# Projecting the first token group from unnormalised x, with the first convolution tap on ScalarE and history copies on GpSimd

## The chip, the cores and the metric

The kernel runs on one core of a Trainium2 chip. The metric is device time in microseconds of one execution. One execution was also recorded by the hardware profiler; its busy times, waits and clocks are what the rows below show. TensorE (PE) multiplies, VectorE (DVE), ScalarE (ACT) and GpSimd (POOL) compute elementwise, SyncE (SP) issues most DMAs, and ScalarE issues the others.

## The reference, cut to what matters

One layer of a hybrid encoder for 2048 prompt tokens and 8 x 16 sample tokens, 17 tiles of 128 tokens in all, width 1024, float32:

```python
h = rmsnorm(x, norm_mix_pre)              # x * rsqrt(mean(x*x)) * gain
P = h @ w_in                              # 3592 columns: q,k,v | z | b,a | B,C,H
qkv = silu(causal_dwconv(P[q,k,v], conv_prev, conv_qkv_w))      # 4 taps
q, k = l2norm(q) * 128**-0.5, l2norm(k)   # per head, 4 heads of 128
beta, g = sigmoid(b), -exp(a_log) * softplus(a + dt_bias)
o, S = gated_delta_rule(q, k, v, g, beta, S0)                   # scan over the tokens
o = rmsnorm(o, gdn_norm_w) * silu(z)
y = B * causal_dwconv(C * H, sc_prev, conv_sc_w)                # 3 taps
x = x + rmsnorm(concat(o, y) @ w_o, norm_mix_post)
x = x + rmsnorm(swiglu(rmsnorm(x, norm_ffn_pre)), norm_ffn_post)
```

The row factor `rsqrt(mean(x*x))` is one number per token, so it can be applied to a token's row of x or to its row of `x*gain @ w_in`. The outputs are the layer's x, the last rows before the convolutions (the history of the next call) and the state S.

## The kernel before, in words

The first stage goes over the tokens in six groups of up to three tiles (`GROUPS`): the first holds prompt tiles 0 and 1 and the sample tile 16. Tokens lie along the free dimension (384 columns), channels along the partitions. Matmuls keep float32 accuracy by a split: x and each weight have a high part, rounded to the fast matmul type, and a low part, the rest; `mm3` (L136) multiplies high by high, low by high and high by low. One projection (`project`) of 128 output channels is 8 x 3 matmuls of 384 columns into one of three PSUM banks (`psd`), and a group has 28 of them: 4 k, 4 v, 4 q, 4 z, and four times C, H, B of the short convolution.

`x_first` (L214 ff.) makes the parts of x for the first group: it loads eight blocks of 128 channels, squares them on ScalarE and VectorE in turn (L227, L229), adds pairs (L232) and sums them over the partitions with one-column matmuls (L234). `rstd` takes the power -0.5 on GpSimd (L130), and `spread` (L171 ff.) turns the row factors into a tile `rb` that has them in all partitions, through a matmul with ones (L178) and a copy (L180). Then each block is multiplied by `rb` (L240), its high part is written by ScalarE with the gain as scale (L243) and its low part by VectorE (L244). Later groups use `x_prep`, which the change leaves as it is.

Weights come through `fetch` and `weights` (L327 ff.). In the first group a raw weight is loaded in two halves (`wr`, three buffers); ScalarE casts each half (L338), GpSimd subtracts for the first half's low part and VectorE for the second's (L340), and the split weight (1 MB, three buffers) is stored to HBM (L343). Later groups load it ready made (L332). Seven of the 28, those with `j % 4 == 3`, are split again in the second group and stored only then; in the last group every second weight is split from raw.

`conv_qkv` (L369 ff.) is the 4-tap convolution: the last three columns of the group before (`hist`) are copied ahead of the projection's columns in a tile R, ScalarE copies the columns out of PSUM, `hist` is renewed from R's end, the tap of weight 3 starts `acc`, and `taps` (L367) adds the other three. The sample tile has its own tile Rs with eight streams of 16 tokens and its own history. A SiLU on ScalarE ends it. `sc_stage` (L448 ff.) does the like with two copies of history and three taps. `gate_prep` (L249 ff.) computes decay and beta for the group, `pair_stage` the k k^T and q k^T blocks and a serial ladder of small products on VectorE, `level_stage`, `chunk_stage` and `sample_stage` the scan.

After the six groups come the output projection and the feed-forward, which the change leaves as they are. The order on each engine's queue is set by a planner: it simulates the program written below in order and places each instruction by the time its inputs are expected, so an instruction can stand well ahead of or behind its place in the text. Each engine takes its own queue strictly in that order.

Of the kernel before, what the change touches and what calls it, by code (L numbers as in the profile page):

```python
# [9 lines left out]
F32 = mybir.dt.float32  # L10
# [15 lines left out]
NS = 8  # L26
# [9 lines left out]
NPD, NPT, NPG = 3, 2, 2  # L36
NR, NKV = 3, 3
# [32 lines left out]
def kernel(  # L70
# [44 lines left out]
    nc.scalar.dma_start(out=cst[:, 0:256], in_=consts[:, 0:256])  # L115
# [25 lines left out]
    with ExitStack() as ph:  # L141
# [30 lines left out]
        def spread(r, n):  # L172
            c = n * P
            rg = small.tile([P, W1], F32, tag="rg", name="rg", bufs=1)
# [4 lines left out]
            rb = small.tile([P, W1], F32, tag="rb", name="rb", bufs=1)  # L179
            A.copy(rb[:, :c], ps[:, :c])  # L180
            return rb
# [33 lines left out]
        def x_first(tiles):  # L215
# [3 lines left out]
            ps = tbank()  # L219
            for k in range(KD):  # L220
                raw = ubuf[k] if k < len(ubuf) else gp.tile([P, H, P], F32, tag="dt", name="dt", bufs=2 * MAXT)
                raw = raw.rearrange("p h c -> p (h c)")[:, :c]
                raws.append(raw)
                (nc.sync if k < 6 else nc.scalar).dma_start(out=raw, in_=xs0[k])
                xk = cp.tile([P, W1], F32, tag="xk", name="xk", bufs=3)
                if k % 2:
                    V.tensor_mul(xk[:, :c], raw, raw)  # L227
                else:
                    A.activation(xk[:, :c], raw, AF.Square)  # L229
                sqs.append(xk)  # L230
                if k % 2:
                    V.tensor_add(xk[:, :c], xk[:, :c], sqs[k - 1][:, :c])  # L232
                    for i in range(n):
                        T.matmul(ps[:, 2 * i:2 * i + 1], xk[:, i * P:(i + 1) * P], ones[:, 0:1], start=(k == 1 and i == 0),  # L234
                                 stop=(k == KD - 1 and i == n - 1), skip_group_check=True)
            r = rstd(small, ps[:, :2 * n].rearrange("p (t c) -> p t c", c=2)[:, :, 0], n, 1.0 / D, EPS, "x")
            rb = spread(r, n)
# [10 lines left out]
            return hi, lo  # L248

        def gate_prep(tiles, hi, lo):  # L250
# [6 lines left out]
            A.activation(bsb[:, :c], ps[:16, :c], AF.Identity, scale=gsct[:, 0:1], bias=gbia[:, 0:1])  # L257
# [111 lines left out]
        def conv_qkv(tiles, ci, ps, dst):  # L369
# [6 lines left out]
            if npr:  # L376
                R = cp.tile([P, 3 + W1], F32, tag="R", name="R", bufs=NR)
                V.tensor_copy(R[:, 0:3], hist[:, ci, :])
                A.copy(R[:, 3:3 + pc], ps[:, :pc])
                V.tensor_copy(hist[:, ci, :], R[:, pc:pc + 3])  # L380
                V.tensor_scalar_mul(acc[:, :pc], R[:, 3:3 + pc], w[:, 3:4])
                taps(acc[:, :pc], lambda d: R[:, d:d + pc], w, 4, pc)
            if npr < n:
                Rs = cp.tile([P, NS, 3 + LS], F32, tag="Rs", name="Rs")
                V.tensor_copy(Rs[:, :, 0:3], cch[:, ci])
                A.copy(Rs[:, :, 3:], ps[:, pc:c].rearrange("p (s l) -> p s l", s=NS))
                V.tensor_copy(cch[:, ci], Rs[:, :, LS:LS + 3])
                V.tensor_scalar_mul(acc[:, pc:c].rearrange("p (s l) -> p s l", s=NS), Rs[:, :, 3:], w[:, 3:4])
# [9 lines left out]
        def qkv_stage(tiles, hi, lo, gt, pool):  # L398
# [6 lines left out]
            for h in range(H):  # L405
                raw = cp.tile([P, W1], F32, tag="kvT", name="kraw", bufs=NKV)
                conv_qkv(tiles, 4 + h, project(h, hi, lo, c), raw)
# [14 lines left out]
            for h in range(H):  # L422
                raw = cp.tile([P, W1], F32, tag="kvT", name="vraw", bufs=NKV)
                conv_qkv(tiles, 8 + h, project(4 + h, hi, lo, c), raw)
# [5 lines left out]
            for h in range(H):  # L430
                o = pool.tile([P, W1], F32, tag="qT", name="qT", bufs=H)
                conv_qkv(tiles, h, project(8 + h, hi, lo, c), o)
# [7 lines left out]
        def z_stage(tiles, hi, lo, gt):  # L440
            c = len(tiles) * P
            sz = gp.tile([P, H, W1], F32, tag="sz", name="sz")
            for h in range(H):
                ps = project(12 + h, hi, lo, c)
                A.activation(sz[:, h, :c], ps[:, :c], AF.Silu)
            gt["sz"] = sz

        def sc_stage(tiles, hi, lo):  # L448
# [4 lines left out]
            for b in range(4):  # L453
# [3 lines left out]
                A.copy(cs[:, :c], pC[:, :c])  # L457
                pH = project(17 + 3 * b, hi, lo, c)
                acc = cp.tile([P, W1], F32, tag="acc", name="acc", bufs=3)
                if npr:  # L460
                    u = cp.tile([P, 3 + W1], F32, tag="R", name="u", bufs=NR)
                    V.tensor_copy(u[:, 0:2], shist[:, b, :])
                    V.tensor_mul(u[:, 2:2 + pc], cs[:, :pc], pH[:, :pc])
                    V.tensor_copy(shist[:, b, :], u[:, pc:pc + 2])
                    V.tensor_scalar_mul(acc[:, :pc], u[:, 2:2 + pc], w[:, 2:3])
                    taps(acc[:, :pc], lambda d: u[:, d:d + pc], w, 3, pc)
                if npr < n:
                    us = cp.tile([P, NS, 3 + LS], F32, tag="Rs", name="us")
                    v = lambda a: a[:, pc:c].rearrange("p (s l) -> p s l", s=NS)
                    V.tensor_copy(us[:, :, 0:2], sch[:, b])  # L470
                    V.tensor_mul(us[:, :, 2:2 + LS], v(cs), v(pH))
                    V.tensor_copy(sch[:, b], us[:, :, LS:LS + 2])
                    V.tensor_scalar_mul(v(acc), us[:, :, 2:2 + LS], w[:, 2:3])
                    taps(v(acc), lambda d: us[:, :, d:d + LS], w, 3, 0)
                pB = project(18 + 3 * b, hi, lo, c)
                yo = cp.tile([P, W1], F32, tag="cs", name="yo")
                V.tensor_mul(yo[:, :c], acc[:, :c], pB[:, :c])
# [190 lines left out]
        hi, lo = x_first(GROUPS[0])  # L668
        fetch()
        late()  # L670
# [32 lines left out]
        for gi, tiles in enumerate(GROUPS):  # L703
            if gi:
                hi, lo = x_prep(tiles)
            gt = gate_prep(tiles, hi, lo)
            qkv_stage(tiles, hi, lo, gt, gp if (len(GROUPS) - gi) % 2 else dp)
            pair_stage(tiles, gi, gt)
            level_stage(tiles, gt)
            z_stage(tiles, hi, lo, gt)  # L710
# [5 lines left out]
            sc_stage(tiles, hi, lo)  # L716
# [559 lines left out]
```

## Time and profile before

| | us |
|---|---|
| median of 3 runs | 2669.16 |
| lowest, highest | 2666.46, 2670.29 |
| span of the profiled execution (first to last instruction) | 2659.7 |
| median of the runs less that span | 9.5 |
| TensorE busy in the span | 2533.2 |
| VectorE, ScalarE, GpSimd busy | 1717.3, 971.8, 939.5 |

No time of the profiled execution beside its span is given; the rows' times belong to that span. The six groups fill about the first 1050 us of it. A busy share is an average over stages with different limits; the stretches below are what can be read for this change.

### The profile page before, as it was taken

What the parts mean: (1) busy time and instruction counts of PE and PEld (TensorE: products, weight loads), DVE (VectorE), ACT (ScalarE), POOL (GpSimd) and SP (SyncE); (2) the same over time, 40 slices, a digit from 0 to 9 for tenths busy, and PEclk for the clock granted to TensorE, in tenths of its full rate; (3) what the DMA queues carried; (4) which work ended last, traced back from release to release, by engine and by line L of the source; (5) the groups of instructions that cost most, each with busy time, mean ns of one, the idle gap of its engine ahead of it and who ended that gap; (6) DMA issues with size and microseconds to landing.
All of it is one profiled execution on the core that took longest, in us unless ns stands there. A gap on an engine that the chain in (4) does not pass through costs nothing.

```text
span 2659.7 us, 42363 instructions
## 1 busy us (share of the span) xinstructions
PE 2533.2 (95%) x15129; PEld 2357.1 (89%) x15129; DVE 1717.3 (65%) x3403; ACT 971.8 (37%) x2337; POOL 939.5 (35%) x841
## 2 busy tenths in 40 slices
PE   7989899999999989999999999999899999999997
PEld 6889789989899987878999999999899987887776
DVE  7788567667575875676978863433633344677698
ACT  5535115142251524433434432222323335333343
POOL 2321001000010210224556654443544445555563
PEclk9999989999999998999999999999999999999999
DMA  6876576666657555667877777877888852443365
GB/s 206 293 255 243 166 245 216 226 225 239 214 207 248 177 182 173 230 214 250 309 261 271 265 259 250 282 247 240 286 287 278 276 169 87 129 123 119 126 217 176
DMA packets 322403, 589.46 MB, mean 222 GB/s; under 512 B 57116, under 2 KB 206304, under 8 KB 303376
## 3 DMA queue, kind: packets, MB, share of 16 engines
q1 hardware_dynamic: 193600, 510.01, 56.7%
q10 hardware_dynamic: 128592, 76.74, 9.5%
q8 instruction: 120, 1.97, 0.3%
q14 instruction: 91, 0.75, 0.1%
HBM read 424.60 MB, written 162.05 MB: 221 GB/s over the span
## 4 chain that ended last, share of the span: by engine, by line
PE 67%; DVE 13%; DMA 8%; issue 4%; ACT 3%; POOL 2%; SPq 1%; ACTq 1%; DVEq 0%; POOLq 0%
PE fbank L963 28%; PE dbank L136 16%; PE fbank L1122 10%; PE tbank L758 3%; PE dbank L758 3%; DMA w<-wsplit 2%; DMA wr<-in_w_in 1%; DVE acc L367 1%; DVE xl L894 1%; POOL dw L829 1%; DMA dr<-in_w_dn 1%; DVE xr L1137 1%; DVE acc L1081 1%; DVE acc L1136 1%; DMA xt<-in_x 1%
## 5 line engine op out<-in xcount | busy, mean ns | idle before, releaser
L963 PE MATMUL fbank<-xh,fw 128*128 128x384 f32 (+1 forms) x3696 | 904.2, 327 | 19.7 <-ACT m L999 12.1
L136 PE MATMUL dbank<-hi,w 128*128 128x384 f32 (+1 forms) x2688 | 691.9, 336 | 16.6 <-DMA w<-wsplit 9.7
L963 PEld LDWEIGHTS fbank<-xh,fw 128*128 128x128 f32 x3696 | 654.9, 189 | 23.4 <-ACT m L999 14.2
L963 PE MATMUL fbank<-xl,fw 128*128 128x384 f32 (+1 forms) x1848 | 604.2, 327 | 0.0
L136 PEld LDWEIGHTS dbank<-hi,w 128*128 128x128 f32 x2688 | 484.8, 193 | 22.8 <-POOL w L340 8.4
L1122 PE MATMUL fbank<-dw,as 128*128 128x512 f32 x1980 | 463.2, 395 | 14.3 <-ACT dw L827 5.0
L1122 PEld LDWEIGHTS fbank<-dw,as 128*128 128x128 f32 x1980 | 372.0, 189 | 105.2 <-DVE acc L1081 7.4
L136 PE MATMUL dbank<-lo,w 128*128 128x384 f32 (+1 forms) x1344 | 449.5, 335 | 0.0
L963 PEld LDWEIGHTS fbank<-xl,fw 128*128 128x128 f32 x1848 | 348.9, 189 | 0.0
L136 PEld LDWEIGHTS dbank<-lo,w 128*128 128x128 f32 x1344 | 259.0, 193 | 1.7 <-issue 0.8
L1106 POOL TENSOR_TENSOR as<-ar,as 128x256 fp32r<-128x256 f32 (+1 forms) x207 | 188.2, 918 | 171.8 <-ACT as L1103 170.4
L939 POOL TENSOR_TENSOR fw<-rg,fw 128x512 fp32r<-128x512 f32 x124 | 176.5, 1424 | 180.9 <-ACT fw L938 180.7
L1081 DVE TENSOR_TENSOR acc<-acc,fbank 128x512 f32<-128x512 f32 x248 | 166.6, 682 | 99.6 <-PE fbank L1122 79.6
L1103 ACT CAST as<-ar 128x256 fp32r<-128x256 f32 (+1 forms) x288 | 118.3, 427 | 181.8 <-PE fbank L1122 132.7
L340 POOL TENSOR_TENSOR w<-wr,w 128x512 fp32r<-128x512 f32 x49 | 78.3, 1599 | 223.6 <-ACT w L338 188.0
L938 ACT CAST fw<-rg 128x512 fp32r<-128x512 f32 x124 | 77.5, 625 | 185.1 <-PE fbank L963 147.9
L367 DVE SCALAR_TENSOR_TENSOR acc<-R,cw,acc 128x384 f32<-128x384 f32 (+1 forms) x216 | 131.0, 609 | 2.0
L1007 DVE TENSOR_TENSOR u<-m,fbank 128x384 f32<-128x384 f32 (+1 forms) x66 | 34.8, 528 | 143.3 <-PE fbank L963 130.4
L1008 POOL TENSOR_TENSOR m<-m,m 128x384 f32<-128x384 f32 (+1 forms) x66 | 69.4, 1051 | 159.5 <-ACT m L1001 119.0
L939 POOL TENSOR_TENSOR fw<-ru,fw 128x512 fp32r<-128x512 f32 x62 | 92.3, 1488 | 85.8 <-ACT fw L938 70.2
L1012 DVE TENSOR_TENSOR c<-u,fbank 128x384 f32<-128x384 f32 (+1 forms) x66 | 34.9, 528 | 127.8 <-PE fbank L963 127.6
L552 POOL MEMSET AU<- 32x128 f32 x16 | 3.2, 197 | 281.0 <-PE gbank L538 272.1
(322 smaller groups left out, 3807.2 us busy)
## 6 DMA issues: line engine op xcount, KB each, us to landing
w<-wsplit SPq DMA_DIRECT2D x119, 1024.0 KB, 6.0
fw<-fsplit SPq DMA_DIRECT2D x188, 512.0 KB, 4.7
fsplit<-fw SPq DMA_DIRECT2D x94, 512.0 KB, 4.1
partd<-pt ACTq DMA_DIRECT2D x88, 384.0 KB, 6.0
rg<-in_w_gu SPq DMA_DIRECT2D x62, 512.0 KB, 3.7
wsplit<-w SPq DMA_DIRECT2D x28, 1024.0 KB, 4.7
wr<-in_w_in SPq DMA_DIRECT2D x98, 256.0 KB, 4.4
ar<-partd SPq DMA_DIRECT2D x48, 384.0 KB, 3.3
```

The lines of the kernel that those rows point to most:

```text
L136: T.matmul(ps, l, r, start=(i == 0), stop=(i == n - 1))
L340: e.tensor_tensor(out=wl[:, c], in0=wr, in1=wh[:, c].bitcast(F32), op=ALU.subtract)
L367: V.scalar_tensor_tensor(acc, raw(d), w[:, d:d + 1], acc, op0=ALU.mult, op1=ALU.add)
L758: T.matmul(pss[n], m_[:, j, :], w_[k][:, n * 512:(n + 1) * 512], start=(k == 0 and ci == 0), stop=(k == KD - 1 and ci == 2))
L938: A.copy(w[:, 0], v)
L939: e.tensor_tensor(out=w[:, 1], in0=v, in1=w[:, 0].bitcast(F32), op=ALU.subtract)
L963: T.matmul(ps, w_[:, c], b_[k][:, :hw], start=(first and k == 0 and ci == 0), stop=(k == KH - 1 and ci == 2), skip_group_check=not first)
L1008: G.tensor_tensor(out=s7, in0=s7, in1=s5, op=ALU.add)
L1081: V.tensor_add(dst, dst, ps)
L1103: ins = A.copy(a[:, 0, :n], v)
L1106: e.tensor_tensor(out=a[:, 1, :n], in0=v, in1=a[:, 0, :n].bitcast(F32), op=ALU.subtract)
L1122: T.matmul(ps, a[:, x_, q * P:(q + 1) * P], w[:, y_], start=(start and q == 0 and ci == 0), stop=(q == c - 1 and ci == 2), skip_group_chec ...
```

## The change

1. In the first group, `x_first` forms high and low parts from unnormalised x times the gain. The sums of squares move to a new function `x_scale`, called after the first projection in program order; it squares in place and returns `rb`. Evictions of the first group's projections multiply by `rb`: `put` for q, k, v and C, and extra multiplications for z, the gates, and the short convolution (C again, which stands for H, and `acc`, which stands for B).
2. The eight loads of x alternate between the queues of SyncE and ScalarE (before: six and two). The first weight is fetched after the second of them, and the constants that hold the identity and the ones are loaded after the eight.
3. `LATE` names ten weights that are split again in the second group, in place of seven.
4. The first tap is an activation on ScalarE with the tap as its scale (read from PSUM for the prompt columns of q, k, v when `rb` is None, from R, Rs, u or us otherwise). History copies are on GpSimd, in all groups.

```diff
+LATE = (0, 1, 2, 4, 6, 8, 10, 18, 22, 26)
-    nc.scalar.dma_start(out=cst[:, 0:256], in_=consts[:, 0:256])
...
 def x_first(tiles):
...
-                (nc.sync if k < 6 else nc.scalar).dma_start(out=raw, in_=xs0[k])
...
-            for k in range(KD):
-                raw = raws[k]
-                V.tensor_mul(raw, raw, rb[:, :c])
...
+                (nc.scalar if k % 2 else nc.sync).dma_start(out=raw, in_=xs0[k])
+                if k == 1:
+                    fetch()
                 l = hp.tile([P, W1], F32R, tag="lo", name="lo")
                 h = hp.tile([P, W1], F32R, tag="hi", name="hi")
                 A.activation(h[:, :c], raw, AF.Copy, scale=g_pre[:, k:k + 1])
...
+        def x_scale(tiles, raws):
+            for k in range(KD):
+                sq = raws[k]
+                if k % 2:
+                    V.tensor_mul(sq, sq, sq)
+                else:
+                    A.activation(sq, sq, AF.Square)
+                sqs.append(sq)
+                if k % 2:
+                    V.tensor_add(sq, sq, sqs[k - 1])
...
+            r = rstd(small, ps[:, :2 * n].rearrange("p (t c) -> p t c", c=2)[:, :, 0], n, 1.0 / D, EPS, "x")
+            return spread(r, n)
...
 def weights(j, gi):
-            late = j % 4 == 3
+            late = j in LATE
...
+        def put(dst, src, rb, lo, hi):
+            if rb is None:
+                A.copy(dst, src[:, lo:hi])
+            else:
+                V.tensor_mul(dst, src[:, lo:hi], rb[:, lo:hi])
 def conv_qkv(tiles, ci, ps, dst, rb):
-                V.tensor_copy(R[:, 0:3], hist[:, ci, :])
-                A.copy(R[:, 3:3 + pc], ps[:, :pc])
-                V.tensor_copy(hist[:, ci, :], R[:, pc:pc + 3])
-                V.tensor_scalar_mul(acc[:, :pc], R[:, 3:3 + pc], w[:, 3:4])
+                G.tensor_copy(R[:, 0:3], hist[:, ci, :])
+                put(R[:, 3:3 + pc], ps, rb, 0, pc)
+                G.tensor_copy(hist[:, ci, :], R[:, pc:pc + 3])
+                A.activation(acc[:, :pc], R[:, 3:3 + pc] if rb is not None else ps[:, :pc], AF.Copy, scale=w[:, 3:4])
...
 def z_stage(tiles, hi, lo, gt, rb):
+                if rb is not None:
+                    V.tensor_mul(sz[:, h, :c], src, rb[:, :c])
 def sc_stage(tiles, hi, lo, rb):
-                A.copy(cs[:, :c], pC[:, :c])
+                put(cs[:, :c], pC, rb, 0, c)
+                if rb is not None:
+                    V.tensor_mul(cs[:, :c], cs[:, :c], rb[:, :c])
...
+                if rb is not None:
+                    V.tensor_mul(acc[:, :c], acc[:, :c], rb[:, :c])
                 V.tensor_mul(yo[:, :c], acc[:, :c], pB[:, :c])
...
-        hi, lo = x_first(GROUPS[0])
+        hi, lo, raws = x_first(GROUPS[0])
+        nc.scalar.dma_start(out=cst[:, 0:256], in_=consts[:, 0:256])
         fetch()
+        first = [project(0, hi, lo, W1)]
+        rb = x_scale(GROUPS[0], raws)
```

`spread` keeps its result in the tile that held the diagonal, with two buffers in place of one each. The bias and scale of the gates come after a multiplication by `rb`.

## Rows read from the trace of the kernel before

**Rows 1.** Busy us of each engine by stretch: granted clock, DMA share, GB/s last.
```profile
0.00:40.00 40.00, 22.63 (x96) 18.95 (x97) 22.22 (x47) 14.10 (x27) 9.35 (x15) 1.00 0.59 196
40.00:160.00 120.00, 112.49 (x670) 109.52 (x669) 99.93 (x288) 66.53 (x164) 38.81 (x29) 0.99 0.80 275
160.00:320.00 160.00, 142.50 (x938) 129.36 (x938) 116.42 (x300) 59.44 (x164) 29.00 (x29) 0.93 0.63 218
...
480.00:640.00 160.00, 156.91 (x1125) 150.49 (x1124) 107.23 (x299) 53.54 (x153) 12.06 (x14) 1.00 0.67 226
...
960.00:1060.00 100.00, 87.20 (x593) 77.75 (x592) 66.84 (x146) 33.01 (x77) 12.65 (x14) 0.86 0.53 171
```
The columns are the stretch, its length, then PE, PEld, DVE, ACT and POOL with instruction counts.

**Rows 2.** The same view, projection line L136 alone (PE, PEld).
```profile
0.00:20.00 20.00, 0.00 (x0) 0.00 (x0) 1.00 0.76 240
20.00:40.00 20.00, 15.00 (x67) 12.78 (x68) 1.00 0.41 151
```

**Rows 3.** Chain of waits, 60 to 180 us, its shares by line.
```profile
by line: DMA wr<-in_w_in 24.6%; PE dbank L136 9.8%; DMA sa<-AU 6.8%; DMA xk<-in_xT 5.9%; DVE acc L367 5.3%; ACT w L338 4.3%; DVE w L340 4.1%; POOL w L340 3.9%; issue 3.6%; DVE lo L209 2.6%; DMA As<-sa 2.6%; DMA xt<-in_x 2.3%; ACT L390 2.1%;
```

**Rows 4.** Instructions in order of time, first 40 us: start, duration, instruction, [idle before].
```profile
3.64 0.52 ACT L229 ACTIVATE xk<-ubuf 128x384 f32<-128x384 f32 x1 [0.69 <-DMA ubuf<-in_xs]
...
5.46 8.22 SPq L337 DMA_DIRECT2D wr<-in_w_in  x4
...
11.85 1.48 POOL L340 TENSOR_TENSOR w<-wr,w 128x512 fp32r<-128x512 f32 x1 [10.95 <-DMA wr<-in_w_in]
...
13.79 1.44 PE L234 MATMUL tbank<-cst,xk 128*128 128x1 f32 x6 [2.61 <-DVE xk L232]
...
17.93 1.65 PE L178 MATMUL tbank<-rg,cst 128*128 128x384 f32 x2 [2.70 <-DVE rg L175]
...
19.62 0.48 ACT L180 COPY rb<-tbank 128x384 f32<-128x384 f32 x1 [2.94 <-PE tbank L178]
...
21.57 2.26 ACT L243 ACTIVATE hi<-ubuf,vec 128x384 fp32r<-128x384 f32 x4
...
25.58 2.19 DVE L244 SCALAR_TENSOR_TENSOR lo<-ubuf,vec,hi 128x384 fp32r<-128x384 f32 x4
...
26.24 0.50 PE L136 MATMUL tbank<-lo,wba 128*16 128x384 f32 x1 [2.55 <-DVE lo L244]
...
28.14 0.84 PE L136 MATMUL dbank<-hi,w 128*128 128x384 f32 x2
...
34.52 0.51 PE L136 MATMUL dbank<-hi,w 128*128 128x384 f32 x2
...
37.93 0.17 DVE L380 COPY hist<-R 128x3 f32<-128x3 f32 x1 [8.04 <-ACT R L379]
```

**Rows 5.** DMA issues, 0 to 340 us: size, median us from issue to landing.
```profile
wr<-in_w_in SPq DMA_DIRECT2D x69, 256.0 KB, 5.2
```

**Rows 6.** Instructions by line and shape, VectorE, 0 to 300 us: busy, mean ns.
```profile
L380 DVE COPY hist<-R 128x3 f32<-128x3 f32 x24 | 5.0, 210 | 12.6 <-ACT R L379 12.4
...
L381 DVE TENSOR_SCALAR acc<-R,cw 128x256 f32<-128x256 f32 x12 | 4.2, 347 | 0.7 <-ACT vraw L390 0.6
...
L388 DVE TENSOR_SCALAR acc<-Rs,cw 128x128 f32<-128x128 f32 x12 | 3.4, 279 | 0.0
L387 DVE COPY cch<-Rs 128x24 f32<-128x24 f32 x12 | 3.1, 261 | 0.1
...
L463 DVE TENSOR_TENSOR u<-cs,dbank 128x256 f32<-128x256 f32 x4 | 1.6, 408 | 0.0
```

**Rows 7.** VectorE in order of time, 9 to 20 us.
```profile
9.13 0.56 DVE L232 TENSOR_TENSOR xk<-xk 128x384 f32<-128x384 f32 x1
...
12.31 1.43 DVE L232 TENSOR_TENSOR xk<-xk 128x384 f32<-128x384 f32 x1
```

**Rows 8.** GpSimd's waits, 320 to 1060 us: total, times, longest.
```profile
POOL AU L552 <- PE gbank L538: 261.8, 13, 62.2
...
POOL kl L603 <- PE gbank L606: 85.5, 6, 28.1
```

More of the change, by code (lines that the diff above doesn't have):

```diff
@@ L178, in spread @@
             T.matmul(ps[:, :c], ones, rg[:, :c], start=True, stop=True)
-            rb = small.tile([P, W1], F32, tag="rb", name="rb", bufs=1)
-            A.copy(rb[:, :c], ps[:, :c])
-            return rb
+            A.copy(rg[:, :c], ps[:, :c])
+            return rg
         def x_prep(tiles):
@@ L223, in x_first @@
                 raws.append(raw)
-                (nc.sync if k < 6 else nc.scalar).dma_start(out=raw, in_=xs0[k])
[L225 to L237, printed above, removed]
-            for k in range(KD):
-                raw = raws[k]
-                V.tensor_mul(raw, raw, rb[:, :c])
+                (nc.scalar if k % 2 else nc.sync).dma_start(out=raw, in_=xs0[k])
+                if k == 1:
+                    fetch()
                 l = hp.tile([P, W1], F32R, tag="lo", name="lo")
@@ L247, in x_first, with gate_prep @@
                 lo.append(l)
-            return hi, lo
-        def gate_prep(tiles, hi, lo):
+            return hi, lo, raws
+        def x_scale(tiles, raws):
+            n = len(tiles)
+            sqs = []
+            ps = tbank()
+            for k in range(KD):
[7 more added lines that the diff above has]
+                    V.tensor_add(sq, sq, sqs[k - 1])
+                    for i in range(n):
+                        T.matmul(ps[:, 2 * i:2 * i + 1], sq[:, i * P:(i + 1) * P], ones[:, 0:1], start=(k == 1 and i == 0),
+                                 stop=(k == KD - 1 and i == n - 1), skip_group_check=True)
+            r = rstd(small, ps[:, :2 * n].rearrange("p (t c) -> p t c", c=2)[:, :, 0], n, 1.0 / D, EPS, "x")
+            return spread(r, n)
+        def gate_prep(tiles, hi, lo, rb):
             n = len(tiles)
@@ L384, in conv_qkv @@
                 Rs = cp.tile([P, NS, 3 + LS], F32, tag="Rs", name="Rs")
[L385 to L388, printed above, removed]
+                G.tensor_copy(Rs[:, :, 0:3], cch[:, ci])
+                sv = lambda a: a[:, pc:c].rearrange("p (s l) -> p s l", s=NS)
+                if rb is None:
+                    A.copy(Rs[:, :, 3:], sv(ps))
+                else:
+                    V.tensor_mul(Rs[:, :, 3:], sv(ps), sv(rb))
+                G.tensor_copy(cch[:, ci], Rs[:, :, LS:LS + 3])
+                A.activation(acc[:, pc:c].rearrange("p (s l) -> p s l", s=NS), Rs[:, :, 3:], AF.Copy, scale=w[:, 3:4])
                 taps(acc[:, pc:c].rearrange("p (s l) -> p s l", s=NS), lambda d: Rs[:, :, d:d + LS], w, 4, 0)
@@ L406, in qkv_stage @@
                 raw = cp.tile([P, W1], F32, tag="kvT", name="kraw", bufs=NKV)
-                conv_qkv(tiles, 4 + h, project(h, hi, lo, c), raw)
+                conv_qkv(tiles, 4 + h, first.pop(0) if first else project(h, hi, lo, c), raw, rb)
                 ps = tbank()
@@ L705 @@
                 hi, lo = x_prep(tiles)
[L706 to L707 removed]
+                rb = None
+            gt = gate_prep(tiles, hi, lo, rb)
+            qkv_stage(tiles, hi, lo, gt, gp if (len(GROUPS) - gi) % 2 else dp, rb, first)
             pair_stage(tiles, gi, gt)
             level_stage(tiles, gt)
[L710 removed]
+            z_stage(tiles, hi, lo, gt, rb)
             for i, t in enumerate(tiles):
```

39 lines of the change are left out of this document (22 added, 17 removed).

## The prediction

> **What bounds the kernel now.** I read the table of stretches first. From 40 to 160 us, where the first token group's projections run, TensorE is busy 112.5 of 120 us, and from 480 to 640 us, a middle group, 156.9 of 160 [rows 1]. The reader should see that the stage is paced by TensorE except in three places: the first 40 us (22.6 busy), 160 to 320 us (142.5 of 160) and the last group's tail from 960 us (87.2 of 100). What follows the stage, out-projection and feed-forward, is untouched. So only idle TensorE time in those places can be won, and whatever brings the projections forward is carried to the end as long as VectorE and the weight loads keep up: VectorE has 99.9 of 120 us busy in the second row, and DMA is at 0.80 there.
>
> Then the same table for the projection line alone: by 40 us, 67 matmuls of L136 have run, all after 20 us [rows 2]. Then the chain of waits from 60 to 180 us: a quarter of it is raw weights landing, a tenth projection matmuls [rows 3]; so the loads run close behind TensorE. Last the instructions in order of time for the start [rows 4]: the first row of x is on chip at 3.6 us, its square begins at once, but normalisation makes everything wait for the last row: last sums of squares at 13.8, spread over the partitions at 17.9, factor copied at 19.6, then eight scalings, the high parts from 21.6 and the low parts from 25.6. TensorE's steady stream begins at 26.24, and the first convolution's work on VectorE (the history copy) at 37.9. The matmuls there first follow each other in 0.32 us (0.84 for a pair, its end included), later in 0.17 (0.51 for a pair): 384 columns at the two levels of the clock, 1.2 and 2.4 GHz, the slow one after TensorE had stood nearly still.
>
> **Start: projection of unnormalised x.** Now high and low parts need only x and the gain. x row 0 at 3.6, high 0.57 (2.26 for four), low 0.55 (2.19 for four) [rows 4]: ready at 4.8. The first weight is asked for after two x rows, at about 2 instead of 5.46. Its halves land a median 5.2 us after issue [rows 5], 7.2; cast, priced from the 0.48 copy of 384 columns as 0.64 for 512; low half on GpSimd 1.48: 9.3. So TensorE starts in earnest at 9.3. Projection 0 takes 24 x 0.32 = 7.7, to 17.0; the last x row (2.1 MB in all at the 196 GB/s of the first stretch is 10.7 us, plus 1.1 for the two parts) does not hold it up. To reach the 67 matmuls of 40 us, 43 more are needed: 43 x 0.17 = 7.3. New in the stream are the sums of squares and the spread, which before ran on an idle TensorE: 4 x 1.44 + 1.65 = 7.4 at the slow clock, 3.7 at the fast one. Sum: 28.0 to 31.7, I take 30. Gain 10 us (8 to 12). If the first weight is no earlier than now (subtraction at 11.85), TensorE starts at 13.3 and the gain is 4; that is the lower end. Upper end: the row factor needs eight lows more on VectorE (4.4 us) ahead of or among the squares, so it is ready at 20.1 (now) to 24, and the first convolution can start 14 to 17 us earlier than 37.9. I take 10, nearest to what the matmul rows give.
>
> The constants' load moves behind the x rows on ScalarE's queue; they are first used by the sums of squares, which now come later, so nothing. The x rows are split four and four over two queues: the loads issue no later than now, nothing to half a us.
>
> **VectorE in the first group.** Removed per convolution [rows 6]: two history copies at 0.21, first tap 0.35, two sample history copies at up to 0.26, sample tap 0.28: 1.57 x 12 = 18.8; the four short convolutions likewise 6.3; eight scalings of x, priced as the lows at 0.55, 4.4. Together 29.5. Added: multiplications at eviction, priced as 0.41 for 256 columns from PSUM and 0.28 for 128, 0.69 each: 12 in q/k/v, 4 in z, 12 in the short convolution (the C factor twice, once before the last product), 1 in the gates: 29 x 0.69 = 20. Net 9.5 us less of some 125. Lower bound 0 (the copies still cost VectorE, next paragraph), upper 9.5. In groups 1 to 5 each convolution saves about 0.8. TensorE is 98% busy there, so I count nothing for it between 320 and 960; at 160 to 320 and in the tail, with 17.5 and 12.8 us of idle TensorE, I take 2 us together (0 to 8).
>
> A row on the copies: the addition L232 takes 0.56 us at 9.13 and 1.43 at 12.31, while a GpSimd subtraction runs from 11.85 to 13.33; it ends 0.4 after that one [rows 4, 7]. So VectorE can be held by a running GpSimd instruction. The Trainium skill ("SBUF — State Buffer", section "Who interferes with whom") says that a VectorE instruction with two SBUF inputs contends with a GpSimd instruction that reads SBUF, and the later one waits to the end of the earlier. The taps left on VectorE have two SBUF inputs, the moved copies read SBUF. By that rule the copies' 0.94 us per convolution come back as blocked taps, VectorE's net turns from 9.5 less to about 5 more in this group, and the sum would be 2659 instead of 2657; it also speaks against the larger gain below.
>
> **ScalarE and GpSimd.** ScalarE gives its eviction copies of the first group to VectorE and takes first taps of the same sizes: even. Later groups give it 16 taps at 0.48: 7.7 us on a load of 53.5 in 160 [rows 1]: nothing as it has cover; without cover a tap delays its convolution by 0.5. A convolution's PSUM bank is now read twice, 0.5 us longer, with three banks of 24 x 0.17 = 4.1 us each: hidden. GpSimd gets 32 copies per group, 64 in the first; the trace has none of this size on it, so between 0.1 and the 0.86 us by which L232 was held; I take 0.25: 8 us in 160, where it is busy 12.1. Queued behind such a copy are weight subtractions and the small powers, for which VectorE waits. But a copy also waits behind those in front of it: see the second rival.
>
> **Weights kept from a later group.** Ten of 28 instead of seven are split anew in the second group and stored only then. In the first group 18 stores of 1 MB instead of 21: 3.1 MB less, 11 us of DMA at the 275 GB/s of 40 to 160; of the first twelve only five are stored, now nine. That is what lets weights follow a stream that starts 10 us earlier: a limit by bytes would move by 11 too. Later weights store 13 of 16 (now 12). In the second group three more stores and raw weights instead of ready ones: 1.5 MB more at a DMA share of 0.63, three more subtractions of 1.5 us on GpSimd, busy 29 of 160: I count 0 (0 to 4 lost). One more weight is fetched ahead throughout, in the same three buffers: 0 to 2 won, counted 0.
>
> **Sum.** 10 + 2 = 12 us off. The profiled span is 2659.7, so 2648 after; the median of the runs, 2669.2, lies 9.5 above it, which I take as unchanged: **2657**, own range 2650 to 2664.
>
> **Rivals.** *A: the early start is starved.* TensorE begins early, then waits for weights 1 to 3 (three raw buffers, freed by GpSimd's 1.5 us) and stays longer at the slow clock. For it: a quarter of the chain is landing weights. Against: four fewer stores among the first twelve weights, none for the first three. Gain 4: 2665.
> *B: GpSimd's order decides.* Its queue is strictly in order, and it stands waiting up to 62 us for level-stage matmuls and up to 28 us in front of the state update's product [rows 8]. A history copy queued behind one holds the taps, then the R buffers, then, when all three banks are full (12.3 us), TensorE. One stall of 28 in each group costs 28 - 12.3 = 16; if the next group has 10 us of slack from other matmuls, 5 remain, times five is 25 minus 12 won: slower by 13, 2682. It decides from a wait of over 12 us. For: the waits are there. Against: they are mostly GpSimd having nothing else to do; the first history copy reads only last group's columns and can go early.
> *C: VectorE's convolutions pace the first group.* At 83% busy, their start 14 to 17 us earlier and 9.5 us less work move the ladder of small products and what hangs on it by 20 or more, and the tail wins 3: 2646. Against: TensorE has only 25 us of idle time in the first 160 [rows 1].
>
> **How the numbers follow.** Forecast 0.58, A 0.17, B 0.08, C 0.17. What can be told from no change is 0.2%, 5.3 us: below 2663.8 is faster. The forecast's 0.58 are nearly all faster (0.56), C all, A 0.04: 0.77. Same: 0.13 of A and 0.02 of the forecast, 0.15. Slower: B, 0.08. The range takes in A's price with 3 us beyond, 2668, and below most of C, 2644; it leaves out B and some of C.
>
> **What would show it.** L136 before 20 us with 25 or more matmuls and over 100 by 40; the first history copy or PSUM multiplication of a convolution by 24 us; VectorE in 40 to 160 down or equal; the boundary of the groups 10 us earlier at 160, 480 and 960 alike. If the 10 us are there at 40 and gone at 320, the second group's extra splits or the ladder took them; if TensorE's idle time before L136 grows in 320 to 960 with GpSimd named as releaser of taps, B holds. The prediction is wrong if TensorE does not start before 13 us.

## The result, and the profile after

The median went from 2668.53 us (20 runs) to 2673.64 us (20 runs): the ratio is 1.0019, 95% interval 1.0011 to 1.0028. That is 5.1 us more, inside the 0.2% that I had called no change and on the other side of what I forecast (2657, range 2644 to 2668). In all that follows one execution, of e2 below, was far off (12555 us), and e2's time and ratio are without it.

The two recorded executions differ by 20 us in span (2659.7 and 2679.7), four times the medians. Before's is near its fastest (2661.5 with what lies around the span), after's is the slowest of its 20 (2681.5). Most of this lies where the change touches nothing: from the first out-projection matmul to the end, before takes 1649.2 us and after 1663.1. The instructions there are the same, but their order isn't quite: the planner placed some 40 of those on VectorE, ScalarE and GpSimd otherwise. Six recorded kernels, before among them, that share before's order on these engines but for up to three instructions take 1649.2 to 1656.7, and e18, which shares after's but for five, takes 1656.0. So these 14 us are in good part one execution against another. What the change did is read from the first stage, which ends at 1010.5 before and 1016.6 after.

The stretches after, to be set beside [rows 1]:

```profile
0.00:40.00 40.00, 31.40 (x161) 27.92 (x162) 27.80 (x57) 21.52 (x40) 18.06 (x36) 0.96 0.65 211
40.00:160.00 120.00, 111.96 (x657) 108.85 (x656) 90.72 (x225) 63.60 (x158) 52.23 (x73) 0.97 0.80 268
160.00:320.00 160.00, 135.49 (x886) 121.71 (x885) 104.97 (x244) 63.85 (x176) 44.45 (x57) 0.90 0.59 202
480.00:640.00 160.00, 154.30 (x1093) 148.44 (x1092) 97.39 (x249) 62.35 (x171) 19.02 (x46) 0.97 0.65 224
```

TensorE wins 8.8 busy us in the first 40 and gives 7.0 back between 160 and 320 (142.5 before). VectorE in 40 to 160 fell from 99.9 to 90.7, and in the first 40 us, where it now has more to do, it rose from 22.2 to 27.8. The projection line alone, to be set beside [rows 2]:

```profile
0.00:20.00 20.00, 11.72 (x49) 9.81 (x50) 1.00 0.70 223
20.00:40.00 20.00, 16.99 (x85) 14.66 (x84) 0.91 0.60 200
```

By the starts of its matmuls, 132 have run by 40 us, 67 before. At 65 x 0.17 us that is a lead of 11 us. (The 67th starts at 23.0 instead of 39.9, a lead of 17; the difference went in a stand of TensorE of 2.4 us before 30.3 and a granted clock of 0.70 in 32 to 36.) Followed through the trace, with the gates' matmuls of that line counted:

| L136 matmuls started by | 40 | 160 | 200 | 240 | 280 | 300 | 320 | 480 | 960 us |
|---|---|---|---|---|---|---|---|---|---|
| before | 67 | 618 | 791 | 908 | 1043 | 1070 | 1081 | 1737 | 3919 |
| after | 132 | 670 | 815 | 940 | 1064 | 1064 | 1076 | 1740 | 3884 |

The lead is there up to 280 and gone at 300. Between 276 and 316 us after starts no projection matmul at all; before has the same hole from 291 to 318. So the question was what happens there. After, in order of time (start, duration, engine, line, instruction, idle before):

```profile
5.78 0.69 PE L136 MATMUL dbank<-hi,w 128*128 128x384 f32 x1 [5.78 <-ACT w L345]
...
21.36 0.15 DVE L128 TENSOR_SCALAR xm<-tbank 128x3 f32<-128x3 f32 x1
...
22.48 1.63 DVE L175 TENSOR_TENSOR rg<-cst,xr 128x384 f32<-128x384 f32 x1 [0.97 <-POOL xr L130]
...
28.77 0.47 ACT L179 COPY rg<-tbank 128x384 f32<-128x384 f32 x1
...
29.50 0.42 DVE L380 TENSOR_TENSOR R<-dbank,rg 128x256 f32<-128x256 f32 x1
...
72.15 0.54 DVE L431 TENSOR_TENSOR kt<-tbank,rkr 128x384 f32<-128x384 f32 x1
...
72.75 0.90 PE L435 MATMUL tbank<-cst,kt 128*128 128x128 f32 x3 [4.77 <-DVE kt L431]
...
140.21 0.18 DVE L536 TENSOR_TENSOR pr<-As,Ts 48x31 f32<-48x31 f32 x1 [2.17 <-DMA As<-sa]
...
196.10 1.20 SPq L539 DMA_DIRECT2D sT<-Ts  x1
...
214.91 0.85 SPq L339 DMA_DIRECT2D w<-wsplit  x2
...
257.88 0.52 ACT L407 ACTIVATE qT<-acc 128x384 f32<-128x384 f32 x1 [1.20 <-DVE acc L374]
...
310.46 0.69 DVE L688 TENSOR_TENSOR st<-st,gbank 128x512 f32<-128x512 f32 x1 [1.45 <-PE gbank L685]
...
312.16 0.69 DVE L520 TENSOR_TENSOR AU<-gbank,dt 128x512 f32<-128x512 f32 x1 [1.02 <-PE gbank L516]
...
314.19 1.25 ACT L466 ACTIVATE sz<-dbank 128x384 f32<-128x384 f32 x3 [7.75 <-DVE ot L609]
...
328.88 0.18 DVE L536 TENSOR_TENSOR pr<-As,Ts 48x31 f32<-48x31 f32 x1 [3.01 <-DMA As<-sa]
```

And the same places before:

```profile
71.73 0.54 DVE L414 TENSOR_TENSOR kt<-tbank,rkr 128x384 f32<-128x384 f32 x1
...
139.66 0.18 DVE L511 TENSOR_TENSOR pr<-As,Ts 48x31 f32<-48x31 f32 x1 [0.57 <-DMA As<-sa]
...
188.34 0.32 SPq L514 DMA_DIRECT2D sT<-Ts  x1
...
269.34 0.51 ACT L390 ACTIVATE qT<-acc 128x384 f32<-128x384 f32 x1
...
311.27 0.69 DVE L663 TENSOR_TENSOR st<-st,gbank 128x512 f32<-128x512 f32 x1 [1.44 <-PE gbank L660]
...
312.98 0.69 DVE L495 TENSOR_TENSOR AU<-gbank,dt 128x512 f32<-128x512 f32 x1 [1.02 <-PE gbank L491]
...
330.43 0.18 DVE L511 TENSOR_TENSOR pr<-As,Ts 48x31 f32<-48x31 f32 x1 [7.21 <-DMA As<-sa]
```

The projections are ahead, but k is normalised (the product `kt`) at 72 in both, the first ladder product is at 140 in both, and the first group's chain then runs up to 20 us later: the ladder's result is stored at 196 instead of 188, the first chunk's first product runs at 232.4 instead of 212.1. The second group's last q is nevertheless out of its SiLU (`qT`) at 258.4 instead of 269.9: there the lead is whole. Last comes the sample tile's recurrence (`st`, `kz`, `qz`), whose end is level. 1.7 us after its last state update, in both, stands the first product of the second group's pair stage (`AU`), and from there the second group's ladder starts at 328.9 and 330.4. Of 11 us of lead 1.5 are left. From there to the out-projection after loses 7.6 us more (1010.5 and 1016.6).

The chain of waits after, 130 to 330 us, says what the first group's chain is made of (start, length, what):

```profile
195.68 0.43 DVE acc L374
196.10 6.28 DMA sT<-Ts
202.44 1.11 SPq L555
...
214.38 0.43 SPq L324
214.91 7.33 DMA w<-wsplit
222.29 5.05 PE dbank L136 x19
227.34 0.60 PE gbank L581 x8
...
280.24 1.78 PE gbank L669 x16
282.02 1.80 PE gbank L671 x16
284.12 0.68 DVE st L687
...
289.09 1.78 PE gbank L669 x16
...
308.35 2.07 PE gbank L685 x2
310.42 1.71 PE gbank L516 x8
```

The ladder's last products stand between convolution taps on VectorE; its store takes 6.28; SyncE then issues the small loads of the level stage one after the other; a weight that stands behind them in that queue is asked for at 214.9 and lands at 222.2; TensorE, in order, holds the level stage's second products (L581) behind the projection that waits for it. From 280 on the chain is the sample recurrence alone, 9 us a head, and then the second group's pair products (L516), whose k and q had been ready since 258.

### The profile page after: what moved, and what is told of

The parts are those of the page before. It is cut to its first block, busy times and chain, and to the rows that moved or that the text cites. A ratio compares the mean times of both kernels' runs of the same rounds, so it can differ in the third digit from the quotient of the medians.

```text
span 2679.7 us, 42541 instructions
## 1 busy us (share of the span) xinstructions
PE 2544.3 (95%) x15129; PEld 2365.9 (88%) x15129; DVE 1676.5 (63%) x3103; ACT 1014.6 (38%) x2426; POOL 1003.5 (37%) x1068
## 4 chain that ended last, share of the span: by engine, by line
PE 59%; DVE 13%; DMA 9%; issue 5%; POOL 3%; ACT 3%; SPq 1%; ACTq 1%; DVEq 0%; POOLq 0%
PE fbank L992 26%; PE dbank L136 14%; PE fbank L1151 10%; DMA w<-wsplit 3%; PE dbank L787 2%; PE tbank L787 2%; DVE xl L923 1%; DMA mr<-mixd 1%; DMA dr<-in_w_dn 1%; POOL dw L858 1%; DVE acc L374 1%; DVE acc L1110 1%; ACTq L1068 1%; POOL fw L968 1%; DVE xr L1166 1%
## 5 line engine op out<-in xcount | busy, mean ns | idle before, releaser
L136 PE MATMUL dbank<-hi,w 128*128 128x384 f32 (+1 forms) x2688 | 697.7, 339 | 34.5 <-DMA w<-wsplit 20.2
L136 PEld LDWEIGHTS dbank<-hi,w 128*128 128x128 f32 x2688 | 490.9, 195 | 42.6 <-issue 11.4
L136 PE MATMUL dbank<-lo,w 128*128 128x384 f32 (+1 forms) x1344 | 452.8, 337 | 0.1
L136 PEld LDWEIGHTS dbank<-lo,w 128*128 128x128 f32 x1344 | 262.0, 195 | 2.2 <-DVE lo L228 0.6
L487 POOL COPY shist<-u 128x2 f32<-128x2 f32 x24 | 16.0, 666 | 191.3 <-DVE u L486 180.6
```

Of the source, the lines that this page charges most:

```text
L136: T.matmul(ps, l, r, start=(i == 0), stop=(i == n - 1))
```

## Experiments

All ratios are to the kernel before on the same chip. The first twelve took the change apart and tried its neighbours.

**The parts alone (e1 to e3, e10 to e12).** One text holds both kernels; each part has a switch, and the weights' list stands beside it.

```diff
-START, TAP_A, COPY_G = False, False, False
+START, TAP_A, COPY_G = True, False, False      # e1; e2: False, True, True; e10: tap; e11: copies
-LATE = tuple(range(3, 28, 4))
+LATE = (0, 1, 2, 4, 6, 8, 10, 18, 22, 26)      # e3 (alone), e12 (with the copies)
```

e1: 

> The kernel before with the new start alone (unnormalised projection, x loads split over two queues, row factor at eviction); seven late weights, taps and history copies on VectorE as before. Theory 1 (the start's 11 us are won, and the first group's serial back end, from the ladder of small products to the sample stage, takes them back by 320 us): within 3 us of the kernel before, with more than 110 L136 matmuls by 40 us and no lead at 320 us. Theory 2 (the moved taps and copies cost what the start wins): 8 to 12 us faster than before. Theory 3 (the ten late weights cost it): also faster, by 5 to 12 us.

e2: 

> The kernel before with the first tap on ScalarE and the history copies on GpSimd alone. Theory 1: within 4 us of before. Theory 2: 8 to 15 us slower. Theory 3: no change.

e3: 

> The kernel before with the ten late weights alone. Theory 1 and 2: within 4 us of before. Theory 3: 5 to 12 us slower, with PE waiting for POOL or DMA of weights in the second group (160 to 320 us).

e10: 

> The kernel before with the first tap on ScalarE alone. Theory 2a (the tap is what costs: an added hop to ScalarE's queue before the other taps): 5 to 10 us slower. Theory 2b (the copies cost): within 3 us. Theory 6: anything within 10 us.

e11: 

> The kernel before with the history copies on GpSimd alone. Theory 2a: 0 to 5 us faster, since e4 against the changed kernel says that the copies win 6. Theory 2b: 5 to 10 us slower.

e12: 

> A candidate: the kernel before with the ten late weights and the history copies on GpSimd, without the new start and with the first tap on VectorE. By the parts (late -3.5, copies -6 by e4): 5 to 10 us faster than the kernel before. Theory 6: no sum of parts holds to better than 5 us.

| | median | ratio, 95% interval | against before |
|---|---|---|---|
| e1 start | 2674.06 | 1.0018 (1.0005 to 1.0031) | +5.5 |
| e2 tap and copies | 2673.02 | 1.0021 (1.0007 to 1.0034) | +4.4 |
| e3 late weights | 2664.27 | 0.9987 (0.9974 to 0.9999) | -4.3 |
| e10 tap on ScalarE | 2682.99 | 1.0065 (1.0050 to 1.0081) | +16.2 |
| e11 copies on GpSimd | 2660.64 | 0.9983 (0.9970 to 0.9997) | -6.1 |
| e12 late weights and copies | 2673.72 | 1.0030 (1.0020 to 1.0041) | +7.0 |

The start alone, which was to win 10, costs as much as the whole change; its lead is there at 40 us (137 matmuls) and gone at 320 (1073, before 1081), as the first theory had it. The tap costs 16 alone, the copies win 6. But the parts don't add: two that win alone lose 7 together. Each edit also makes the planner lay out every queue anew, and e9 shows what that is worth.

**Copies back on VectorE (e4)**, in the changed kernel.

```diff
-START, TAP_A, COPY_G = True, True, True
+START, TAP_A, COPY_G = True, True, False
```

> The changed kernel with the history copies back on VectorE (tap on ScalarE, start and ten late weights kept). Theory 1: within 4 us of the changed kernel. Theory 2: 5 to 10 us faster than the changed kernel if the copies are the part that costs. Theory 3: like the changed kernel.

2678.15, ratio 1.0041 (1.0026 to 1.0056): 4.5 us slower than the changed kernel in medians, with intervals that just overlap. Rival B had the copies on GpSimd cost some 25 us; taking them away wins nothing, so B is out.

**The sample tile's recurrence ahead of the prompt tiles' (e5 before, e6 after).**

```diff
-            for i, t in enumerate(tiles):
+            for i, t in sorted(enumerate(tiles), key=lambda it: it[1] != SAMPLE):
```

e5: 

> The kernel before with the sample stage written ahead of the two prompt chunks of the first group. Theory 4 (TensorE's lead is lost at one gate: the second group's z projections fill all three banks and wait for the sz tile that the sample stage's output reads last, at 313 us in both kernels): the sample stage ends earlier, TensorE's hole at 285 to 310 us closes, 8 to 20 us faster than before. Theory 2 (taps and copies): says nothing of it; no change.

e6: 

> The changed kernel with the same reordering. Theory 4: its lead of 50 projection matmuls at 160 us is kept to 320, so it is 5 to 12 us faster than the kernel before with the reordering, and 15 to 25 faster than the changed kernel. Theory 2: still about 5 us behind the kernel before with the reordering.

2674.53 (1.0034, 1.0021 to 1.0046) and 2671.41 (1.0024, 1.0014 to 1.0033). The last `st` update moves to 296 in both, but the second group's first `AU` stays at 311.8 and 310.4: now the prompt tiles' chunks come last. So both expectations of a gain (8 to 20 us, and 15 to 25 over the changed kernel) missed: the gate is the whole of the first group's scan, not the place of one tile in it.

**One more weight fetched ahead before (e7), one less after (e8).**

```diff
         hi, lo = x_first(GROUPS[0])
         fetch()
+        fetch()
```

e7: 

> The kernel before with one weight more fetched ahead (one more call of fetch before the groups), nothing else. Theory 5 (the deeper prefetch, which the changed kernel has throughout, puts weight loads in front of other transfers on SyncE's queue): 3 to 8 us slower. Theory 4: within 3 us.

e8: 

> The changed kernel without the second fetch before the first projection, so that the prefetch is as deep as before. Theory 5: 3 to 8 us faster than the changed kernel. Theory 4: within 4 us of it.

2675.28 (1.0036, 1.0022 to 1.0050) and 2675.63 (1.0042, 1.0030 to 1.0054). Neither is better than its kernel, so the lead isn't lost for want of a weight. The 9.7 us that e7 costs are more than theory 5 said, but its counterpart e8 wins nothing.

**A reordering that changes no work (e9).** The loads of the two sample histories are written after those of the gate's constants.

```diff
-        nc.scalar.dma_start(out=cch, in_=cache_c)
-        nc.scalar.dma_start(out=sch, in_=cache_s)
...
+        nc.scalar.dma_start(out=cch, in_=cache_c)
+        nc.scalar.dma_start(out=sch, in_=cache_s)
```

> A control: the kernel before with the two small loads of the convolution caches written after the gate and w_ba loads. No work is added or removed; the planner's order moves. Theory 6 (the planner's fixed order, chosen for expected times, moves with every edit, and that alone is worth about 5 us): 3 to 10 us off the kernel before, likely slower. All other theories: within 2 us of it.

2673.23, ratio 1.0022 (1.0008 to 1.0036): 6.5 us more for nothing. A difference of 5 or 6 us between two kernels of this planner is therefore no evidence on the work that the edit changes. The 16 us of the tap (e10) and the 15 us between e13 and e14 below are more than that, but one control doesn't show how far orders can differ.

**Without the sample recurrence (e13 before, e14 after).** Its state loads, the padded k and q, its matmuls and the new state are left out (state_s isn't written); its o is v. The state is four loads and four stores of 512 KB, 4 MB and not the 8 that I expected to save.

```diff
-            for h in range(H):
-                st = wk.tile([P, NS, P], F32, tag="st", name="st", bufs=2)
...
+            G.tensor_copy(o, gt["vt"][:, :, i, :])
```

e13: 

> The kernel before with the sample tile's state recurrence left out (its state loads, zero-padded k and q, all its matmuls and the new state; its o is v, and state_s is not written). Every theory: some 20 to 50 us less than the kernel before, as 8 MB of state less move and some 300 small matmuls with their VectorE work are gone. It is the partner of e14.

e14: 

> The changed kernel with the same part left out. Theory 'sample stage': the lead of the start dies at 310 us because the z projections of the second group hold all PSUM banks until the sample tile's last output is out; without that output this kernel is 6 to 12 us faster than e13. Theory 'serial chain': the first group's chain (row factor, gates, k normalisation, ladder, level, chunks) is no earlier than before, so the two stand within 5 us of each other, or this one up to 8 slower, as the whole kernels do.

2641.61 (0.9909, 0.9893 to 0.9925) and 2626.35 (0.9851, 0.9830 to 0.9871): the change is now worth 15.3 us, where the whole kernels differ by 5.1 the other way. The 'serial chain' theory, as I had put it, missed: although the first group's chain is hardly earlier (ladder stored at 185.4 in e13, at 183.2 in e14), the lead passes on once nothing of the sample tile stands between the groups. The 'sample stage' theory had 6 to 12. The first ladder product of the second group in e13, then in e14:

```profile
297.13 0.18 DVE L511 TENSOR_TENSOR pr<-As,Ts 48x31 f32<-48x31 f32 x1 [0.77 <-DMA As<-sa]
```

```profile
279.60 0.18 DVE L536 TENSOR_TENSOR pr<-As,Ts 48x31 f32<-48x31 f32 x1 [4.54 <-DMA As<-sa]
```

It is 17.5 us apart, against 1.5 in the whole kernels, and the out-projection starts at 980.6 and 967.4. With the recurrence in, the second group's pair products stand behind it on TensorE and VectorE, whatever the projections did; without it they begin at 248.4 and 254.9.

Three limits. The two kernels differ in all parts of the change, so the start's share of the 15.3 isn't shown. The recurrence's `kz` and `qz` also lie in the ladder's buffers (tags `As` and `Ts`), so its place in the queues and its hold on these buffers go together. And the lead isn't steady behind the second ladder: at the third it is 3.7 us (447.3 and 443.6), at the last 10.2.

**The planner off (e15 before, e16 after)**: each queue in the order of the text.

```diff
-TLS = True
+TLS = False
```

e15: 

> The kernel before with the planner off: each queue has the order of the program text. Every theory: slower than before, by 20 to 200 us, as little is overlapped across stages. It is the partner of e16.

e16: 

> The changed kernel with the planner off. Theory 'order': the lost time is the planner's new order, not the changed work; in text order the earlier start is worth its 8 to 12 us, and this one is that much faster than e15. Theory 'work': the first tap on ScalarE's queue costs in any order; this one is level with e15 or up to 15 us slower.

2802.90 (1.0519, 1.0494 to 1.0544) and 2799.63 (1.0497, 1.0478 to 1.0516): overlapping. The lead at 40 us is 53 matmuls (132 and 79), 22 at 200. 4 us of it are left at the out-projection (1085.6 and 1089.7). So the lost gain is not the planner's order alone; the plain order of the text loses most of it too, but elsewhere. Here the recurrence ends at 242.7 and 231.5, long before the second group's pair products (323.0 and 309.1), and the second ladder starts 15.3 us apart, in e15 and then e16:

```profile
341.23 0.18 DVE L511 TENSOR_TENSOR pr<-As,Ts 48x31 f32<-48x31 f32 x1 [4.05 <-DMA As<-sa]
```

```profile
325.92 0.18 DVE L536 TENSOR_TENSOR pr<-As,Ts 48x31 f32<-48x31 f32 x1 [7.79 <-DMA As<-sa]
```

The ladder of the fifth group has nothing left of it (868.9 and 868.7). So the stop at the recurrence belongs to the planner's layout, and there is a second loss further on, which no run here explains.

**The second group's z projections after its short convolution (e17 before, e18 after).** In the rows above ScalarE's SiLU of z waits 7.75 us for the sample tile's output `ot`, which reads the one `sz` tile, and by then the z projections hold all three PSUM banks. This edit moves them.

```diff
-        order = [(j, gi) for gi in range(len(GROUPS)) for j in range(28)]
+        order = [(j, gi) for gi in range(len(GROUPS)) for j in
+                 ((*range(12), *range(16, 28), *range(12, 16)) if gi == 1 else range(28))]
...
+            if gi == 1:
+                sc_stage(tiles, hi, lo)
             z_stage(tiles, hi, lo, gt)
...
-            sc_stage(tiles, hi, lo)
+            if gi != 1:
+                sc_stage(tiles, hi, lo)
```

e17: 

> The kernel before with the second group's z projections written (and their weights fetched) after its short convolution; all else as it was. Theory 'sample stage': the projections that held the three PSUM banks until 314 us now find a free tile, TensorE does not stand at 300 to 320 us, and some 5 to 10 us are won: 2657 to 2663. Rival 'order noise': any reordering moves this kernel by some 6 us either way, and this does no more.

e18: 

> The changed kernel with the same edit. Theory 'sample stage': the lead of the start now passes 310 us, so this is 6 to 15 us faster than e17 and the fastest of all that compute the whole reference: some 2647 to 2656; the count of projection matmuls is ahead of e17's at 320, 480 and 640. Rival: the sample recurrence itself (VectorE and small matmuls in 260 to 310), not the wait of z, holds the second group; then this stands within 5 us of e17.

2677.14 (1.0036, 1.0024 to 1.0048) and 2682.86 (1.0065, 1.0048 to 1.0081): both slower, and the theory that these banks hold the second group missed. In e18 by stretch (columns as in the first table):

```profile
280.00:320.00 40.00, 40.00 (x242) 37.60 (x242) 18.09 (x31) 6.01 (x16) 5.10 (x10) 1.00 0.82 280
320.00:480.00 160.00, 141.79 (x987) 131.70 (x985) 92.00 (x241) 60.37 (x160) 20.66 (x40) 0.95 0.55 190
```

The hole at 280 to 320 is closed (32.0 busy of 40 in after) and the lead lives on at 320 (1229 matmuls, e17 1191, after 1076). But the short convolution's matmuls now stand among the recurrence's, which ends at 343 instead of 310; the second group's ladder starts at 364.6 (e17: 343.8), and TensorE idles 18 us in 320 to 480 (6.5 in after). Filled with early projections, the hole moved behind the ladder.

Set side by side, first ladder product of the second group and start of the out-projection:

| | before | after | e1 | e3 | e11 | e9 | e10 | e13 | e14 | e17 | e18 |
|---|---|---|---|---|---|---|---|---|---|---|---|
| ladder | 330.4 | 328.9 | 332.5 | 328.2 | 321.6 | 334.7 | 337.5 | 297.1 | 279.6 | 343.8 | 364.6 |
| out-projection | 1010.5 | 1016.6 | 1018.1 | 1006.3 | 1004.7 | 1024.1 | 1022.9 | 980.6 | 967.4 | 1012.3 | 1022.3 |

In these kernels, with the projections in their old places, the out-projection comes 678 to 689 us after this ladder; e17 and e18, with projections done ahead, 658 to 669. The others under the planner spread wider, from 672.7 (e8) to 697.8 (e5), so the ladder's start alone doesn't set the end. With the recurrence in, no kernel with the early start (after, e1, e18; also e4 at 331.5, e6 at 322.1, e8 at 339.8) has an earlier ladder than the best without it (e11, 321.6).

The fastest of all that compute the whole reference, and faster than both kernels, is e11, the copies alone: 2660.64, 0.17% under before (interval 0.03 to 0.30%). By e9 that may be its order more than its copies.

## Why the prediction was wrong

**The start** did what I said, and more. TensorE's first projection ran at 5.78 us (forecast 9.3) and 132 matmuls by 40 us (over 100). The lead was 11 us where I took 10. The 67th matmul, which I had put at 30, started at 23.0: the start came 3.5 us earlier, the sums of squares took 2.8 us instead of 5.8, and the spread came after it. This step was right, and rival A, the starved start, is out.

**The step that failed** is in my first part: "whatever brings the projections forward is carried to the end as long as VectorE and the weight loads keep up". I read the busy share of TensorE as what paces the group. A group also has a chain (gates, k's norm, ladder, level, chunks, sample) whose end, in the planner's order, lets the next group's pair stage in, and 98% busy TensorE only says that projections fill the time around it. In the first group, which alone holds the sample tile, that chain ends last in both kernels: the second group's q is ready at 269.9 before and 258.4 after, and its pair products come at 311.0 and 310.2, behind the recurrence. The 17.5 us of idle in 160 to 320, which I had counted as room to win 2 more, was the sign: the longest wait of TensorE there, 7.4 us in all, is that of the recurrence's last products (L660) for `ye`. I had named the sign, a lead at 40 that is gone at 320, but gave it to the second group's splits or the ladder; the ladder's store is 8 us late, but the lead ends at the scan behind it. The term of 10 was worth nothing, and TensorE lost 7.0 where I had added 2. e14 shows a gain once the recurrence is out, 15.3 us for the whole change. That the same step would have paid in the whole kernel without this stop is argued, not shown: in text order the lead gets past the place and is lost later.

**The row factor** was the other half of it. I had it ready at 20.1 to 24 and the first convolution 14 to 17 us earlier than 37.9. The sums of squares stand among the weights' subtractions on VectorE and GpSimd (`rg` takes 1.63 us beside a subtraction at 22.41) and the copy stands behind casts on ScalarE, at 28.8; the first eviction is at 29.5, so 8 us earlier. And by `kt` at 72 even these are gone: k's first head leaves its SiLU at 39.4 (before 43.9), but its transpose on TensorE runs at 60.4 (before 62.7). After stands still there, for a transpose that waits for `kt`, and pays for it in clock (granted clock third from last):

```profile
64.00:68.00 4.00, 3.98 (x23) 1.00 0.95 326
68.00:72.00 4.00, 0.00 (x0) 0.99 0.95 356
72.00:76.00 4.00, 3.25 (x12) 0.50 0.62 225
76.00:80.00 4.00, 4.00 (x17) 0.65 0.81 274
```

The columns here are the stretch, its length, PE alone, then the clock. In the 12 us from 68 on TensorE starts 29 matmuls, before 71. At 0.50 it runs at 1.2 GHz, the lower of its two levels, after a stand of 5 us.

**VectorE's work** fell somewhat more than worked out: by an estimate from the traces' durations, the instructions taken out of the first group had some 30 us, and the multiplications take 18.4 (I had 29.5 and 20). That 40 to 160 us alone lost 9.2 is no test of the 9.5, since part of the group's work moved ahead of 40. By line and shape, 0 to 300 us, beside [rows 6]:

```profile
L374 DVE SCALAR_TENSOR_TENSOR acc<-R,cw,acc 128x384 f32<-128x384 f32 x36 | 23.8, 664 | 15.3 <-ACT acc L394 14.8
...
L380 DVE TENSOR_TENSOR R<-dbank,rg 128x256 f32<-128x256 f32 x12 | 5.0, 414 | 0.8 <-PE dbank L136 0.4 <-POOL Rs L398 0.4
...
L380 DVE TENSOR_TENSOR cs<-dbank,rg 128x384 f32<-128x384 f32 x4 | 2.2, 544 | 0.0
```

But the ladder began at 140 as before, so rival C, which saw VectorE's convolutions as the pace and the ladder 20 us earlier, fell with the forecast.

**The tap** I put at even, or 0.5 us a convolution without cover. After, VectorE waits for it (waits of VectorE, 0 to 1010 us: total, times, longest):

```profile
DVE acc L374 <- ACT acc L394: 53.5, 30, 9.2
```

The other three taps stay on VectorE, and the first one now comes from a queue with casts, SiLUs and table loads in front of it. That e10 is slower is measured (+16 us, more than the one control moved); that this wait is how, is only argued, for in e10 itself VectorE's wait for the tap is 13.9 us in all.

**GpSimd.** Rival B was wrong. Long waits are still there, the longest sum now in front of a copy, beside [rows 8] (320 to 1060 us):

```profile
POOL shist L487 <- DVE u L486: 168.5, 16, 26.3
POOL AU L577 <- PE gbank L563: 87.7, 14, 15.5
...
POOL kl L628 <- PE gbank L631: 24.0, 5, 19.7
```

They end with work that isn't there yet, as I had argued. Whether the copies win is open: they did in e11, in after against e4 and in e2 against e10 (6.1, 4.5 and 10.0 us), and lost 9.5 in e12 against e3. I had them at 0.25 us; by line over the first stage (busy, mean ns):

```profile
L393 POOL COPY hist<-R 128x3 f32<-128x3 f32 x72 | 23.0, 320 | 115.7 <-ACT R L378 108.3 <-DVE R L380 5.5 <-DMA wr<-in_w_in 1.1
...
L391 POOL COPY R<-hist 128x3 f32<-128x3 f32 x72 | 19.3, 271 | 110.3 <-DVE acc L374 92.8 <-DVE rkm L128 4.6 <-DVE cr L285 3.4
```

By the Trainium skill ("SBUF — State Buffer", section "Who interferes with whom") I had put 2 us against the sum for copies that contend with taps. Some copies do take 1.2 to 1.3 us instead of 0.3, as one at 73.15 us (1.32) beside a subtraction on VectorE, so the rule can be seen in a row; in the time 2 us can't be told from an order, e11 is 6 faster, and the rule decides nothing here.

**Weights kept.** e3 and e12 lie on both sides of before, so I can say no more than that the edit moves less than an order does. TensorE's waits for ready weights rose, 20.2 us against 9.7 over the span's projections; one of them, at 222 us, is in the chain above.

**The 9.5 us** that I added between span and median were wrong as an offset: a run's time is its span and 1.8 us (2681.5 and 2679.7). The rest was that the recorded run had been a fast one.

What stays open: where the lead of text order goes and why after loses 7.6 us behind the second ladder; why k, 4.5 us sooner out of its SiLU, is not transposed and normalised sooner by as much (some 20 us pass before its transpose in both), and how the whole kernel's 5 us divide between the tap and the order of the queues.

## What to carry to other kernels

Before an idle engine's gap is counted as won, follow one group's serial chain to the first instruction of the next group that waits for it: if that is not the work you bring forward, the lead can be worth nothing however busy the engine is. Take the suspected gate out altogether, in both kernels, as e13 and e14 do; it tells in two runs whether a gain exists behind it, but takes the gate's buffers and queue places away as well, so follow the lead to the end too. Where a planner lays out the queues, run controls that change no work first (several: one gives a size and no spread), and believe no difference smaller than they make.

## What the runs showed of the hardware

A store of 0.2 MB and the loads that depend on it make a long step: the ladder's result was 6.28 us on its way, and SyncE's issues for the level stage mostly came 0.48 us apart, 11 us for the 20 of them, with a weight load standing behind. GpSimd takes 0.27 to 0.32 us in the mean for a copy of three columns, VectorE 0.21 [rows 6]. The same instructions, in the same order on VectorE, ScalarE and GpSimd but for up to three, took 1649.2 to 1656.7 us in one recorded execution each of six kernels (from out-projection to end), so one profile per kernel can't tell 5 us in 2660.
